# Row dot products in one VectorE instruction at another pace, attention weights turned by transpositions, a convolution begun earlier

## The chip, the cores and the metric

The kernel runs on one core of a Trainium2 chip, as one program from the first load to the last store. The core has four computing engines: TensorE (PE in the profile, its weight loads PEld), VectorE (DVE), ScalarE (ACT) and GpSimd (POOL). SyncE (SP) issues most of the loads. Each engine runs its own instructions in program order and waits on semaphores for the others. The metric is the device time of one execution in microseconds (us), lower is better. Three runs of the kernel before took 2879.74, 2887.54 and 2888.85 us. All order of work is written out by hand: an engine's instructions run in the order in which the code issues them.

## The reference, cut to what matters

Two transformer blocks work one after the other on 512 tokens of width 1024, in float32. The change touches the attention and the convolution of block 1 and the expert layer of block 2.

```python
# block 1, per row of the grid and head: attention over 512 local and 256 context keys
p = softmax(concatenate([s_loc, s_ctx], axis=-1))            # 768 weights for each query
o = einsum('bhqk,bhkd->bhqd', p[..., :n_loc], v_blk) + einsum('bhqk,bhkd->bhqd', p[..., n_loc:], v_ctx)
...
# block 1, conformer convolution: 512 channels, 31 taps over the positions
u = a * sigmoid(g)
y = conv(u, conv_w, width 31, one filter per channel) + conv_b
y = silu(layernorm(y, ln_g, ln_b)) @ w_out
...
# block 2, expert layer: 8 heads x 16 = 128 experts per token out of 16384
u = expert_down[eb]                                          # eb: (tokens, 8, 16)
act = gelu(einsum('td,thkd->thk', xb, u)) * gb
out = einsum('thk,thkd->td', act, expert_up[eb])
```

## The kernel before

**Block 1, attention (`attention1`).** Queries stand in 16 pieces, four pairs of heads by four times 128 positions; the loop over them is `seq`, its counter `n`. For each piece TensorE forms the products (tiles `loc`, `cxs`), VectorE adds the bias and finds the least value (`least`), ScalarE takes the exponentials with their sums into `s1` (`exps`), and then the 128 x 768 weights `P` of each of the two heads have to be turned, six blocks of 128 x 128, into `PT` (`turn`), before TensorE multiplies them with the values (`pv`). The division by the sum is done in the turn: `diag` makes a diagonal matrix `d` of the reciprocals on VectorE, and each block is multiplied with `d` as a float32 matrix product. Between these steps TensorE is kept full by `fill1` (for `n` under 8: the convolution's eight inputs `glu(m)` and units of a modulation product, `m1`) and `fill2` (for `n` from 8). Inputs 0 to 3 of `glu` are the four groups of 128 channels of `a` (tile `u`), 4 to 7 the same groups of `g` (tile `g`).

**Block 1, convolution (`conv_steps`).** It runs on VectorE alone, four channel groups by 31 taps, one instruction of 128 x 512 per tap. It is started at `n == 8` by `glu_end` (four sigmoids on ScalarE between two changes of its function table, four products on VectorE) and then doled out, some seven taps per `n`, and in `merge` some nine per column block of `fill3`. `merge` calls `conv.finish()` at its column block 12; the layer norm behind it (`layernorm`) begins with sums over `y`, the convolution's output in tile `g`, on TensorE (helper line L241).

**Block 2, expert layer (`do_peer`).** Of the four groups of 128 tokens three are computed densely: TensorE forms the products of 384 tokens with all expert rows (`score_steps`, tile `pS`, 102 of 128 chunks stored away to memory, `spill`), weights `wH` and `wL` being the two float32r parts of a loaded float32 tile (`Splitter`: `wH` is a copy on ScalarE, L180, `wL` a subtraction, L189, on VectorE or, where `self.sp.low` is "g", on POOL). The fourth group is gathered: each token's 128 rows of `expert_down` are fetched by number, one indirect DMA of 128 rows (one per partition) at a time, into four buffers `rows`, and multiplied with the token's own row `ht` to a dot product. `Gather.tick` does one step of that: POOL issues the fetch of row `n`, multiplies row `n - 2` with `ht` (L2275), and ScalarE sums row `n - 3` (L2278). After 128 rows, `Gather.up` fetches rows of `expert_up` and adds them up on VectorE (L2301).

The layer has three stages. In the **routing stage** (1522 to 1812 us of the trace) TensorE forms the queries and 47 score chunks, while VectorE sorts the best keys (`Route`, tiles `hv`, `oh`, `pf`) for a budget of microseconds per chunk; ticks begin when the first head's row numbers are known. In the **one-hot stage** (1812 to 2185 us) VectorE makes 96 pairs of one-hot matrices `oo` (L2064, two buffers), ScalarE scales them by the gates (L2068), TensorE multiplies them to `pg` (L2084), and the remaining chunks are scored in between; `spent` counts microseconds and calls a tick when its budget is used up. In the **sum stage** (2185 to 2852 us) TensorE multiplies the weighted scores (`A`, split into `AH` and `AL`) with `expert_up` into `acc`; what is left of the gathering is spread evenly over it by `gpace`, which is computed from the ticks already made.

Of the kernel before, what the change touches and what calls it, by code (L numbers as in the profile page):

```python
# [19 lines left out]
T = 512  # L20
# [265 lines left out]
class Kern:  # L286
# [225 lines left out]
    def b1_plan(self):  # L512
# [6 lines left out]
        for m in range(8):  # L519
            self.fill1 += [("in", 12 + m), ("m1", 8 + m)]  # L520
# [277 lines left out]
    def attention1(self, h, qT, kT, v, u_t, g_t, gA, conv, sm):  # L798
# [3 lines left out]
        with tc.tile_pool(name="a1", bufs=1) as a1, tc.tile_pool(name="ps2", bufs=1, space=PSUM) as ps:  # L802
            def glu(m):
                return self.dmaj_steps(("in", 6 + m // 2), h, ps, lambda pt: nc.scalar.copy(
                    u_t[:, m, 15:15 + T] if m < 4 else g_t[:, m - 4], pt))

            def glu_end():
                for m in range(4):
                    nc.scalar.activation(g_t[:, m], g_t[:, m], AF.Sigmoid)
                    V.tensor_tensor(out=u_t[:, m, 15:15 + T], in0=u_t[:, m, 15:15 + T], in1=g_t[:, m], op=OP.mult)  # L810
                nc.scalar.preload_act_table_set("natural_log_exp_and_others")
# [47 lines left out]
            def diag(Ps):  # L859
                ds = []  # L860
                for P, s1 in Ps:
                    V.tensor_tensor(out=s1[:, 2:3], in0=s1[:, 0:1], in1=s1[:, 1:2], op=OP.add)
                    V.reciprocal(s1[:, 3:4], s1[:, 2:3])
                    d = a1.tile([128, 128], F32, name="d", tag="d", bufs=2)
                    V.tensor_scalar(d, self.c("ident"), s1[:, 3:4], None, op0=OP.mult)
                    ds.append(d)
                return ds

            def turn(Ps, ds, fill):

                PTs = []
                for (P, s1), d in zip(Ps, ds):
# [4 lines left out]
                    for c0, c1 in ((0, 4), (4, 6)):  # L877
                        t1 = ps.tile([128, 4, 128], F32, name="t1", tag="tr", bufs=2)
                        for c in range(c0, c1):
                            nc.tensor.matmul(t1[:, c - c0], P[:, c * 128:(c + 1) * 128], d, start=c == c0,  # L880
                                             stop=c == c1 - 1, skip_group_check=True)
# [15 lines left out]
            ds = diag(Ps)  # L897
            for n, (hp, i) in enumerate(seq):
# [10 lines left out]
                PTs = turn(Ps, ds, fill)  # L909
# [3 lines left out]
                if n == 8:  # L913
                    glu_end()
                if n > 8:
                    conv.run(2.4)
                pv(hp, i, PTs)
                if nxt:
                    ds = diag(Ps)
# [3 lines left out]
                if n > 8:  # L923
                    conv.run(2.4)
# [952 lines left out]
    def do_peer(self):  # L1877
# [7 lines left out]
        with ExitStack() as es:  # L1885
# [39 lines left out]
            with ExitStack() as e2:  # L1925
                rt = e2.enter_context(tc.tile_pool(name="rt2", bufs=1))
                i1, i2, gt = [rt.tile([128, 4, 128], F32, name=n) for n in ("i1", "i2", "gt")]
                with ExitStack() as e3:
# [61 lines left out]
                    while True:  # L1990
# [3 lines left out]
                        if s[0] == "d":  # L1994
# [5 lines left out]
                            if s[1] % 6 < 5:  # L2000
# [35 lines left out]
            with ExitStack() as e3:  # L2036
# [11 lines left out]
                def spent(us):  # L2048
# [3 lines left out]
                    if wait > 0:  # L2052
                        G.tick()
                        wait -= 3.7
# [190 lines left out]
class Gather:  # L2245
# [19 lines left out]
    def tick(self):  # L2265
# [7 lines left out]
        if 2 <= n < 130:  # L2273
            u = self.rows[:, (n - 2) % R]
# [249 lines left out]
```

## Time and profile before

| What | Value |
|---|---|
| median of three runs | 2887.54 us |
| the profiled execution, its own time | 2876.13 us |
| its span in the trace | 2874.3 us |
| PE busy | 2687.1 us (93%) |
| DVE busy | 1759.0 us (61%) |
| ACT busy | 1149.6 us (40%) |
| POOL busy | 940.9 us (33%) |
| POOL's 128 row products, L2275 | 318.8 us |

The span reaches from the first to the last instruction; the execution's own time is 1.8 us longer, and lies 11.4 us under the median of the runs. Busy times of different engines overlap. A share of the whole span says little here, since the stages have different limits: each is to be looked at by itself.

### The profile page before, as it was taken

What the parts mean: (1) busy time and instruction counts of PE and PEld (TensorE: products, weight loads), DVE (VectorE), ACT (ScalarE), POOL (GpSimd) and SP (SyncE); (2) the same over time, 40 slices, a digit from 0 to 9 for tenths busy, and PEclk for the clock granted to TensorE, in tenths of its full rate; (3) what the DMA queues carried; (4) which work ended last, traced back from release to release, by engine and by line L of the source; (5) the groups of instructions that cost most, each with busy time, mean ns of one, the idle gap of its engine ahead of it and who ended that gap; (6) DMA issues with size and microseconds to landing.
All of it is one profiled execution on the core that took longest, in us unless ns stands there. A gap on an engine that the chain in (4) does not pass through costs nothing.

```text
span 2874.3 us, 38727 instructions
## 1 busy us (share of the span) xinstructions
PE 2687.1 (93%) x14985; PEld 2073.9 (72%) x14985; DVE 1759.0 (61%) x2830; ACT 1149.6 (40%) x2226; POOL 940.9 (33%) x555
## 2 busy tenths in 40 slices
PE   7999989989999998999899988898889999999998
PEld 4877757654454444778778878788889898888886
DVE  5234884343233334344449998979884667887887
ACT  3245423321111113244444444788884433333333
POOL 2031233310000001002337777888883533222221
PEclk9999999999999999999999998999999999999999
DMA  7235653379989993210136556677876778999994
GB/s 292 70 131 175 223 203 132 148 303 383 420 341 404 420 419 147 75 59 30 45 123 208 193 191 216 215 264 268 299 277 234 280 263 304 340 335 328 335 344 163
DMA packets 189675, 689.66 MB, mean 240 GB/s; under 512 B 16560, under 2 KB 91952, under 8 KB 134832
## 3 DMA queue, kind: packets, MB, share of 16 engines
q1 hardware_dynamic: 151696, 546.10, 50.9%
q0 software_dynamic: 37504, 137.90, 13.8%
q10 hardware_dynamic: 288, 3.15, 0.3%
q8 instruction: 119, 1.95, 0.3%
q14 instruction: 68, 0.56, 0.1%
HBM read 637.67 MB, written 49.41 MB: 239 GB/s over the span
## 4 chain that ended last, share of the span: by engine, by line
PE 42%; DVE 12%; ACT 7%; issue 2%; DMA 0%; POOL 0%; DVEq 0%; ACTq 0%; POOLq 0%; SPq 0%
PE acc L328 6%; PE acc L329 6%; PE acc L327 6%; PE pS L329 3%; PE pS L327 3%; PE pS L328 3%; DVE oo L2064 2%; DVE wL L189 2%; ACT oo L2068 2%; PE pt L327 2%; ACT wH L180 2%; PE pt L328 2%; PE pt L329 1%; PE pg L2084 1%; ACT rows L2278 1%
## 5 line engine op out<-in xcount | busy, mean ns | idle before, releaser
L189 DVE TENSOR_TENSOR wL<-ringA,wH 128x1024 fp32r<-128x1024 f32 x277 | 398.1, 1443 | 198.3 <-ACT wH L180 193.4
L189 POOL TENSOR_TENSOR wL<-ringA,wH 128x1024 fp32r<-128x1024 f32 (+1 forms) x82 | 189.1, 2312 | 915.5 <-PE bc L351 529.5
L180 ACT CAST wH<-ringA 128x1024 fp32r<-128x1024 f32 (+1 forms) x359 | 366.1, 1026 | 56.9 <-PE acc L329 16.9
L329 PE MATMUL pS<-hH,wL 128*128 128x384 f32 x1024 | 349.5, 341 | 30.4 <-DVE wL L189 30.4
L327 PE MATMUL pS<-hH,wH 128*128 128x384 f32 x1024 | 357.5, 349 | 0.6 <-ACT gS L1908 0.6
L328 PE MATMUL pS<-hL,wH 128*128 128x384 f32 x1024 | 348.1, 340 | 0.0
L2275 POOL TENSOR_TENSOR rows<-rows,ht 128x1024 f32<-128x1024 f32 x128 | 318.8, 2491 | 4.6 <-DMA rows<-e_dn,idx 2.3
L328 PE MATMUL acc<-wL,AH 128*128 128x512 f32 x768 | 305.2, 397 | 3.1 <-DVE wL L189 3.0
L327 PE MATMUL acc<-wH,AH 128*128 128x512 f32 x768 | 304.9, 397 | 0.6 <-ACT AH L2180 0.6
L329 PE MATMUL acc<-wH,AL 128*128 128x512 f32 x768 | 304.6, 397 | 0.0
L2256 POOL DMA_INDIRECT rows<-e_up,idx x128 | 145.5, 1137 | 407.3 <-DVE ht L2301 391.8
L2256 POOL DMA_INDIRECT rows<-e_dn,idx x128 | 191.9, 1499 | 128.9 <-ACT rows L2278 106.2
L327 PE MATMUL pt<-hH,wH 128*128 128x512 f32 x512 | 215.3, 420 | 10.1 <-ACT hH L393 7.0
L329 PEld LDWEIGHTS pS<-hH,wL 128*128 128x128 f32 x1024 | 195.3, 191 | 33.0 <-DVE wL L189 33.0
L2064 DVE TENSOR_TENSOR oo<-cst,cl 128x1024 f32<-128x1024 f32 x96 | 209.5, 2209 | 6.8 <-PE pg L2084 6.6
L328 PE MATMUL pt<-hL,wH 128*128 128x512 f32 x512 | 205.7, 402 | 2.4 <-DVE hL L379 2.3
L329 PE MATMUL pt<-hH,wL 128*128 128x512 f32 x512 | 205.8, 402 | 0.5 <-DVE wL L189 0.5
L327 PEld LDWEIGHTS pS<-hH,wH 128*128 128x128 f32 x1024 | 195.9, 191 | 2.7 <-ACT gS L1908 0.9
L328 PEld LDWEIGHTS pS<-hL,wH 128*128 128x128 f32 x1024 | 195.7, 191 | 1.7
L2180 ACT CAST AH<-A 128x384 fp32r<-128x384 f32 x128 | 65.8, 514 | 312.1 <-PE acc L328 263.2
L328 PEld LDWEIGHTS acc<-wL,AH 128*128 128x128 f32 x768 | 144.7, 188 | 38.8 <-DVE wL L189 5.0
L329 PEld LDWEIGHTS acc<-wH,AL 128*128 128x128 f32 x768 | 144.8, 189 | 35.3 <-DVE AL L2184 0.3
(496 smaller groups left out, 5241.4 us busy)
## 6 DMA issues: line engine op xcount, KB each, us to landing
ringA<-t_dn SPq DMA_DIRECT2D x64, 1024.0 KB, 5.7
ringA<-t_up SPq DMA_DIRECT2D x64, 1024.0 KB, 7.3
ringB<-w_eu SPq DMA_DIRECT2D x42, 1024.0 KB, 12.8
ringA<-w_ed SPq DMA_DIRECT2D x39, 1024.0 KB, 9.0
ringB<-w_eg SPq DMA_DIRECT2D x37, 1024.0 KB, 13.3
ringA<-w_in SPq DMA_DIRECT2D x30, 1024.0 KB, 5.2
ringA<-w_eg SPq DMA_DIRECT2D x28, 1024.0 KB, 11.0
ringB<-w_ed SPq DMA_DIRECT2D x27, 1024.0 KB, 8.5
```

The lines of the kernel that those rows point to most:

```text
L180: self.kern.nc.scalar.copy(H, v)
L189: (self.kern.nc.vector if self.low == "v" else self.kern.nc.gpsimd).tensor_tensor(out=L, in0=v, in1=H, op=OP.subtract)
L327: te.matmul(ps, a[0], b[0], start=start, stop=False, skip_group_check=skip)
L328: te.matmul(ps, a[0], b[1], start=False, stop=False, skip_group_check=skip)
L329: te.matmul(ps, a[1], b[0], start=False, stop=stop, skip_group_check=skip)
L2064: V.tensor_tensor(out=oo, in0=iota.unsqueeze(1).unsqueeze(1).to_broadcast([128, 2, 4, 128]), in1=cl[:, 0:2, tok:tok + 4].unsqueeze(3).to_b ...
L2068: nc.scalar.activation(oo[:, 0, t], oo[:, 0, t], AF.Copy, scale=cl[:, 2, tok + t:tok + t + 1])
L2084: nc.tensor.matmul(pg[:, t], o2[:, t], o1[:, t], start=True, stop=True)
L2180: nc.scalar.copy(AH, A)
L2256: k.nc.gpsimd.indirect_dma_start(out=self.rows[:, p % self.R], out_offset=None, in_=k.ap[src], in_offset=bass.IndirectOffsetOnAxis(ap=self ...
L2275: nc.gpsimd.tensor_tensor(out=u, in0=u, in1=self.ht, op=OP.mult)
L2278: nc.scalar.activation(u, u, AF.Copy, accum_out=self.S[:, n - 3:n - 2])
```

## The change

1. `Gather.tick` no longer uses POOL and ScalarE for the dot product. One VectorE instruction multiplies row `n - 3` with `ht` and sums it into `S`. POOL keeps the fetches.
2. The ticks come at another pace: in the routing stage with every second score chunk instead of five of six, in the one-hot stage every 4.2 us of counted work instead of 3.7. By the two programs 31, 63 and 34 of the 128 dot products now stand in the routing, one-hot and sum stages; before it were 47, 71 and 10.
3. `diag` is gone. `scaled` divides `P` by its sum in place, on ScalarE, and `turn` uses transpositions (the constant identity `ident` as the moving operand) instead of products with `d`.
4. `fill1` takes the convolution's inputs in the order 0, 1, 4, 5, 2, 3, 6, 7; `glu_end` is called twice, for channel groups 0 and 1 as soon as four inputs are there, for 2 and 3 as soon as eight are. The convolution is doled out from the `n` after the first call.

```diff
-        for m in range(8):
-            self.fill1 += [("in", 12 + m), ("m1", 8 + m)]
+        for m, i in enumerate((0, 1, 4, 5, 2, 3, 6, 7)):
+            self.fill1 += [("in", 12 + i), ("m1", 8 + m)]
...
-            def glu_end():
-                for m in range(4):
+            def glu_end(ms):
+
+                for m in ms:
                     nc.scalar.activation(g_t[:, m], g_t[:, m], AF.Sigmoid)
+                for m in ms:
                     V.tensor_tensor(out=u_t[:, m, 15:15 + T], in0=u_t[:, m, 15:15 + T], in1=g_t[:, m], op=OP.mult)
                 nc.scalar.preload_act_table_set("natural_log_exp_and_others")
...
-            def diag(Ps):
-                ds = []
+            def scaled(Ps):
+
                 for P, s1 in Ps:
                     V.tensor_tensor(out=s1[:, 2:3], in0=s1[:, 0:1], in1=s1[:, 1:2], op=OP.add)
                     V.reciprocal(s1[:, 3:4], s1[:, 2:3])
-                    d = a1.tile([128, 128], F32, name="d", tag="d", bufs=2)
-                    V.tensor_scalar(d, self.c("ident"), s1[:, 3:4], None, op0=OP.mult)
-                    ds.append(d)
-                return ds
+                for P, s1 in Ps:
+                    nc.scalar.activation(P, P, AF.Copy, scale=s1[:, 3:4])
...
-                            nc.tensor.matmul(t1[:, c - c0], P[:, c * 128:(c + 1) * 128], d, start=c == c0,
-                                             stop=c == c1 - 1, skip_group_check=True)
+                            nc.tensor.transpose(t1[:, c - c0], P[:, c * 128:(c + 1) * 128], self.c("ident"))
...
-                if n == 8:
-                    glu_end()
-                if n > 8:
+                if n > first:
                     conv.run(2.4)
+                if (n >= 8 or first > n) and len(glus) >= 4 * (1 + (n >= 8)) and ends:
+                    first = min(first, n)
+                    glu_end(ends.pop(0))
                 pv(hp, i, PTs)
                 if nxt:
-                    ds = diag(Ps)
+                    scaled(Ps)
                 fill.run(0.5 * us)
                 if left == 1:
                     fill.finish()
-                if n > 8:
+                if n > first:
                     conv.run(2.4)
...
-                            if s[1] % 6 < 5:
+                            if s[1] % 2:
                                 G.tick()
...
-                        wait -= 3.7
+                        wait -= 4.2
...
-        if 2 <= n < 130:
-            u = self.rows[:, (n - 2) % R]
-            nc.gpsimd.tensor_tensor(out=u, in0=u, in1=self.ht, op=OP.mult)
         if 3 <= n:
             u = self.rows[:, (n - 3) % R]
-            nc.scalar.activation(u, u, AF.Copy, accum_out=self.S[:, n - 3:n - 2])
+            nc.vector.scalar_tensor_tensor(u, u, 1.0, self.ht, op0=OP.mult, op1=OP.mult,
+                                           accum_out=self.S[:, n - 3:n - 2])
```

The first place is VectorE in the attention loop where the convolution begins. Before, this is at `n` = 9; the rows run from the first tap (L748) to the taps behind `diag` (L862 to L865).

```order
L748 TENSOR_SCALAR g<-u,prm 128x512
L752 SCALAR_TENSOR_TENSOR g<-u,prm,g 128x512 x3
L862 TENSOR_TENSOR s_2229<-s_2229 128x1
L863 RECIPROCAL s_2229<-s_2229 128x1
L865 TENSOR_SCALAR d<-cst,s_2229 128x128
L862 TENSOR_TENSOR s_2232<-s_2232 128x1
L863 RECIPROCAL s_2232<-s_2232 128x1
L865 TENSOR_SCALAR d<-cst,s_2232 128x128
L752 SCALAR_TENSOR_TENSOR g<-u,prm,g 128x512 x4
```

Of the changed kernel the same place stands at `n` = 5; the sums and reciprocals (now L868, L869) are left.

```order
L748 TENSOR_SCALAR g<-u,prm 128x512
L752 SCALAR_TENSOR_TENSOR g<-u,prm,g 128x512 x3
L868 TENSOR_TENSOR s_1760<-s_1760 128x1
L869 RECIPROCAL s_1760<-s_1760 128x1
L868 TENSOR_TENSOR s_1763<-s_1763 128x1
L869 RECIPROCAL s_1763<-s_1763 128x1
L752 SCALAR_TENSOR_TENSOR g<-u,prm,g 128x512 x4
```

The diagonal is gone from VectorE, and the taps begin four pieces earlier; the two scalings of `P` (128 x 768) stand on ScalarE behind the exponentials.

The second place is VectorE in the middle of the one-hot stage. Before, it had only the one-hot matrices and the subtractions of the weights:

```order
L2064 TENSOR_TENSOR oo<-cst,cl 128x1024 x2
L189 TENSOR_TENSOR wL<-ringA,wH 128x1024
L2064 TENSOR_TENSOR oo<-cst,cl 128x1024 x2
L189 TENSOR_TENSOR wL<-ringA,wH 128x1024
L2064 TENSOR_TENSOR oo<-cst,cl 128x1024 x2
```

In the changed kernel the dot products of the gathered rows (L2280) stand among them:

```order
L2280 SCALAR_TENSOR_TENSOR rows,S<-rows,ht 128x1024
L2069 TENSOR_TENSOR oo<-cst,cl 128x1024
L189 TENSOR_TENSOR wL<-ringA,wH 128x1024
L2280 SCALAR_TENSOR_TENSOR rows,S<-rows,ht 128x1024
L2069 TENSOR_TENSOR oo<-cst,cl 128x1024 x2
L189 TENSOR_TENSOR wL<-ringA,wH 128x1024
L2280 SCALAR_TENSOR_TENSOR rows,S<-rows,ht 128x1024
L2069 TENSOR_TENSOR oo<-cst,cl 128x1024
```

About two of three one-hot matrices now have a dot product next to them on VectorE.

The third place is POOL in the routing stage, where it has fetches and, for every second chunk, a subtraction. Of the changed kernel:

```order
L2261 DMA rows<-e_dn,idx 128x1024 x2
L189 TENSOR_TENSOR wL<-ringA,wH 128x1024
L2261 DMA rows<-e_dn,idx 128x1024 x2
L189 TENSOR_TENSOR wL<-ringA,wH 128x1024
L2261 DMA rows<-e_dn,idx 128x1024 x2
```

And before, with a product behind each fetch:

```order
L2256 DMA rows<-e_dn,idx 128x1024
L2275 TENSOR_TENSOR rows<-rows,ht 128x1024
L189 TENSOR_TENSOR wL<-ringA,wH 128x1024
L2256 DMA rows<-e_dn,idx 128x1024
L2275 TENSOR_TENSOR rows<-rows,ht 128x1024
L2256 DMA rows<-e_dn,idx 128x1024
L2275 TENSOR_TENSOR rows<-rows,ht 128x1024
```

The products are gone from POOL; in the one-hot stage nothing but fetches is left there.

## Rows read from the trace of the kernel before

**Rows 1.** Busy time by stretch: start:end, length, PE, PEld, DVE, ACT, POOL, clock, DMA share, GB/s

```profile
140.00:345.00 205.00, 201.86 (x1658) 147.88 (x1654) 107.60 (x287) 100.44 (x276) 41.95 (x21) 1.00 0.46 159
345.00:400.00 55.00, 54.48 (x361) 39.54 (x364) 53.37 (x49) 20.87 (x43) 24.86 (x11) 1.00 0.76 285
400.00:450.00 50.00, 37.21 (x216) 24.34 (x209) 27.08 (x32) 11.32 (x23) 8.43 (x4) 0.86 0.47 167
1522.00:1812.00 290.00, 259.58 (x1376) 245.07 (x1375) 274.54 (x776) 132.57 (x210) 231.11 (x112) 0.95 0.62 210
1812.00:2185.00 373.00, 325.59 (x1986) 308.77 (x1985) 310.02 (x155) 309.00 (x737) 302.12 (x149) 0.98 0.76 263
2400.00:2852.00 452.00, 452.00 (x1958) 366.49 (x1957) 356.91 (x419) 161.13 (x223) 98.56 (x100) 1.00 0.92 322
```

**Rows 2.** What TensorE waited for in these stretches: total us, times, longest

```profile
PE cs L241 <- DVE g L752: 12.8, 1, 12.8
...
PE pS L329 <- DVE wL L189: 30.4, 8, 10.9
...
PE pg L2084 <- ACT oo L2068: 41.0, 44, 2.9
PE t L2031 <- DVE i L2407: 6.2, 2, 5.6
```

**Rows 3.** Timeline of VectorE and POOL around 1612 us: start, duration

```profile
1612.33 3.54 DVE L189 TENSOR_TENSOR wL<-ringA,wH 128x1024 fp32r<-128x1024 f32 x1
...
1612.37 2.41 POOL L2275 TENSOR_TENSOR rows<-rows,ht 128x1024 f32<-128x1024 f32 x1
```

**Rows 4.** VectorE's groups, routing stage (two), one-hot stage (two): busy us, mean ns

```profile
L189 DVE TENSOR_TENSOR wL<-ringA,wH 128x1024 fp32r<-128x1024 f32 x33 | 59.2, 1806 | 14.0 <-ACT wH L180 13.8 <-issue 0.3
L2404 DVE TENSOR_TENSOR oh<-oh,hif 128x1024 f32<-128x1024 f32 x14 | 27.4, 1996 | 0.0
...
L2064 DVE TENSOR_TENSOR oo<-cst,cl 128x1024 f32<-128x1024 f32 x96 | 209.5, 2209 | 6.8 <-PE pg L2084 6.6
L189 DVE TENSOR_TENSOR wL<-ringA,wH 128x1024 fp32r<-128x1024 f32 x51 | 94.9, 1863 | 52.2 <-ACT wH L180 52.2
```

**Rows 5.** Single lines of the code: min/median/max ns, first and last start

```profile
L2064 DVE TENSOR_TENSOR oo<-cst,cl x96: 1210/1216/4016, 1821.5 to 2167.7; 128x1024 f32<-128x1024 f32 x96
...
L189 POOL TENSOR_TENSOR wL<-ringA,wH x21: 2373/2407/3887, 1524.9 to 1805.9; 128x1024 fp32r<-128x1024 f32 x21
```

**Rows 6.** The same view, for lines like the new dot product

```profile
L1289 DVE SCALAR_TENSOR_TENSOR junk<-srow,cst,grow x32: 741/748/753, 630.2 to 1072.9; 128x512 f32<-128x512 f32 x32
L1289 DVE DVE_READ_ACCUMULATOR junk<-srow,cst,grow x32: 80/84/86, 630.9 to 1073.5; 128x1 f32 x32
...
L2301 DVE SCALAR_TENSOR_TENSOR ht<-rows,S,ht x127: 1276/1279/1287, 2266.2 to 2823.5; 128x1024 f32<-128x1024 f32 x127
```

**Rows 7.** The same view, ScalarE's sum of a row and its exponentials

```profile
L2278 ACT ACTIVATE rows<-rows x128: 1042/1062/1081, 1526.1 to 2259.3; 128x1024 f32<-128x1024 f32 x128
...
L854 ACT ACTIVATE P<-P,m x32: 721/727/740, 141.5 to 328.6; 128x512 f32<-128x512 f32 x32
```

**Rows 8.** Timeline of TensorE: six products with `d`; later eight transpositions in block 2

```profile
158.15 1.60 PE L880 MATMUL t<-d,P 128*128 128x128 f32 x12
159.51 0.47 PE L327 MATMUL pt<-hH,wH 128*128 128x512 f32 x1
...
1253.75 1.03 PE L1663 MATMUL t<-cst,P 128*128 128x128 f32 x8
1254.62 0.28 PE L1643 MATMUL S<-negu,idb 128*128 128x128 bf16 x2
```

**Rows 9.** Convolution taps on VectorE: group from 336 to 424 us, then all

```profile
L752 DVE SCALAR_TENSOR_TENSOR g<-u,prm,g 128x512 f32<-128x512 f32 x82 | 83.9, 1023 | 2.9
...
L752 DVE SCALAR_TENSOR_TENSOR g<-u,prm,g x120: 741/752/2956, 266.1 to 423.3; 128x512 f32<-128x512 f32 x120
```

**Rows 10.** DMA issues, 1522 to 2185 us: count, median us to landing

```profile
rows<-e_dn,idx POOLq DMA_INDIRECT x119, 5.6
```

## What was predicted

> **What bounds the kernel now.** I read the busy times by stretch first, then what TensorE waited for in each, then the instructions that were late. The stretches of [rows 1] show where TensorE is the limit: it is busy 201.9 of 205 us in the attention of block 1 and all 452 us of the sum stage. There only less work for TensorE can help. In three stretches it idles. From 400 to 450 us it works 37.2 us at a mean clock of 0.86; one single wait, of 12.8 us, is named in [rows 2], for the convolution's last tap. In the routing stage it idles 30.4 us, all of it for the subtractions `wL` on VectorE, which is busy 274.5 of 290 us. In the one-hot stage it idles 47.2 us, 41.0 of them for ScalarE's scaled one-hots `oo` and 6.2 for the last routing step.
>
> Why VectorE is so full is seen in [rows 3]: a subtraction begins at 1612.33 us, POOL's product of a gathered row at 1612.37, and the subtraction takes 3.54 us, while lines of its kind and size take 1.2 us alone [rows 5]. It ends about one subtraction after POOL's product does. In [rows 4] the whole groups are stretched: the one-hots of L2064 take 2209 ns in the mean against a median of 1216 for the same line [rows 5] (its worst is 4016), the subtractions 1806 and 1863, the routing's products 1996. So POOL's product doesn't only cost POOL: while it runs, VectorE's instructions with two operands in on-chip memory stand still.
>
> **The change part by part.** *The turn.* A piece's six products with `d` are twelve passes of TensorE; from their start to that of the next instruction it is 159.51 - 158.15 = 1.36 us [rows 8]. Eight transpositions in block 2 take 1254.62 - 1253.75 = 0.87 us, 0.109 each, so six take 0.65. There are 32 turns: 32 x 0.71 = 22.7 us less, on an engine with 98% of this stretch, if the weights are ready. They are now scaled on ScalarE, 128 x 768. No such row exists: 512 columns take 0.73 us, 1024 take 1.06 [rows 7]; I take 0.9 each, 29 us in all, on an engine with 100.4 busy of 205 [rows 1]. The scaling waits for `pv`, the sum and the reciprocal, and is followed by half of the filling work and the next products on TensorE, some 4 us by the stretch's pace (205 us over 16 pieces is 12.8 each); it hides there except at the first piece and where the function table is changed once more. I charge 3 us; from below nothing, from above 0.7 us for each of the 32 turns, which would eat the gain. Sum: -20.
>
> *The convolution* begins four pieces earlier. Seven taps a piece at 0.75 us [rows 9] are 21 us of VectorE's work moved into a stretch where it is busy 107.6 of 205. Before, it is full (53.4 of 55 us) while TensorE comes to the layer norm, and 82 taps took 83.9 us there, 1023 ns each. The layer norm is reached 20 us earlier, but 29 taps fewer are left behind the attention, 29 x 1.02 = 30 us, on top of which VectorE no longer makes `d`. 30 is more than 20, but less than 20 + 12.8, so by this sum 2.8 us of the wait would stay; VectorE's lag at the attention's end is gone too, so I count the wait as removed, -12.8. From below -10; from above -15, since the clock's fall goes with the idle time.
>
> *Routing stage.* Of the 68 long POOL instructions (47 products, 21 subtractions [rows 5]) 47 go. The two groups of this stage in [rows 4] are stretched by 33 x (1.806 - 1.216) + 14 x (1.996 - 1.216) = 30.4 us; 47/68 of that is 21.0. VectorE gets 31 dot products. Their price: a line of the same operation with a sum, 512 wide, takes 748 ns and 84 more to read the sum out; the same operation without a sum, 1024 wide, takes 1279 [rows 6]. So 1.36 us each, 42.2 us. VectorE: 274.5 - 21.0 + 42.2 = 295.7, which is 6 us more than the stage has now. That bound leaves out the smaller groups that are stretched as well. The other bound is that all TensorE's waits go, -30.4. I take the middle, -12.
>
> *One-hot stage.* POOL is left with fetches. The two groups are stretched by 96 x 0.993 + 51 x 0.647 = 128.3 us; 63 dot products cost 85.7. VectorE: 310.0 - 128.3 + 85.7 = 267.4 us. ScalarE loses 71 sums of 1.06 us, of 309.0. Both are then well under TensorE's own 325.6 us, so I count its whole idle time as gone: -47. From above half of it, -24, if the two one-hot buffers keep the three engines in step; from below -60, since TensorE's 325.6 includes filling its pipeline again behind some 46 waits.
>
> *Sum stage.* 24 more dot products and 24 more fetches land here, and the pace rises from (259 - 121)/150 + 0.02 = 0.94 to (259 - 97)/150 + 0.02 = 1.10 steps a chunk. VectorE is busy 357 of 452 us; 0.16 x 1.3 us a chunk over some 107 chunks add 22, to 84%. The DMA's share is 0.92 at 322 GB/s; 0.16 fetches of 0.52 MB a chunk add 9 MB to 145.5, 6%, to 0.98. Both are covered by TensorE's full 452 us: 0. If transfers were full already, 6% of 452 would be 27 us more; that is the upper end.
>
> Together -20 - 12.8 - 12 - 47 = -92. From the profiled execution's 2876.1 that gives 2784; the runs' median lies 11.4 us above that execution, so I predict 2796 for the runs.
>
> **A rule against it.** The new line has two float32 operands in on-chip memory and a sum, and [rows 6] show this form 512 wide at 748 ns, as fast per column as the form without a sum (752 ns [rows 9]). The Trainium skill's page Vector Engine (DVE) Microarchitecture Reference, section Points that are easy to get wrong, says that this operation with two sources in SBUF that aren't bf16 runs at half throughput, as no port is left for the accumulator. By that rule a dot product would take about twice as long; the trace disagrees, and the sum goes by the trace.
>
> **The rivals.** *VectorE stays the bound* in routing (+6) and the one-hot stage gives only half (-24): -33 + 6 - 24 = -51, 2837. For it speaks the sum of 295.7, against it the stretched groups left out. *The scaling comes late at every turn* and eats the 20 us: -72, 2816. For it: ScalarE is in order, and what it does for the filling work stands behind a scaling that waits for VectorE. Against: four microseconds of cover. *The dot product costs double*, 2.64 us: routing 274.5 - 21 + 81.8 = 335, +45; one-hot 310 - 128.3 + 166.3 = 348, -25; in all -13, 2875. Against it speak the 748 ns. *Slower: VectorE now waits for the gather.* It is in order, so a dot product whose row hasn't landed holds the subtractions and one-hots behind it; before, POOL stood there and held nobody on TensorE's path. 94 dot products lie in the two stages; at 0.98 us of wait each the 92 us are gone, at 1.5 us it is +49, 2937. Against it: a fetch lands 5.6 us after its issue [rows 10], and is issued three ticks ahead, some 15 us in the one-hot stage (63 ticks in 326 us). *Better:* routing -30, one-hot -60, 2765. That the row's sum on ScalarE was what TensorE waited for, and not POOL's hold, changes nothing, as both go.
>
> **How the numbers follow.** Forecast 0.60 (2768 to 2815), VectorE stays the bound 0.18, scaling late 0.12, double cost 0.02, late gather 0.04, better 0.04. The range 2768 to 2842 holds the forecast and the first two rivals and leaves out what is beyond. 0.3%, some 9 us, is what runs of this kernel spread and so about what a measurement tells from no change. Faster by more than that: 0.94, within it 0.02, slower 0.04.
>
> **What would show it.** In the profile after: L880's successor at 0.65 us for six transpositions; no wait of L241 for a tap; the one-hots' mean near 1.22 us and `wL` on VectorE near 1.23 in the one-hot stage; TensorE's wait for `oo` under 10 us; the dot product near 1.28 us plus 0.08. The prediction is wrong if the routing stage is longer than 290 us, if VectorE's idle time is put down to the landing of gathered rows, or if the sum stage shows TensorE waiting.

## The result and the profile after

The changed kernel takes 2783.34 us in the median of four runs (2781.31 to 2786.41), the kernel before, on the same chip, 2883.64 (2875.05 to 2888.85): a ratio of 0.9659, 95% interval 0.9633 to 0.9685. The forecast was 2796 us, within 2768 to 2842, and faster. The profiled execution took 2781.99 us with a span of 2780.1, which is 94 us less than before's 2874.3.

The first view is that of [rows 1] for the kernel after, over the stretches that answer to those (all start earlier now); the sixth stretch is the sum stage.

```profile
140.00:340.00 200.00, 185.91 (x1471) 127.39 (x1469) 124.25 (x284) 130.04 (x313) 42.17 (x23) 0.97 0.47 164
340.00:400.00 60.00, 59.87 (x388) 43.81 (x389) 51.02 (x45) 22.02 (x45) 25.44 (x12) 1.00 0.79 288
400.00:450.00 50.00, 49.32 (x309) 34.86 (x309) 7.53 (x16) 19.27 (x38) 9.91 (x6) 1.00 0.50 176
1500.00:1768.00 268.00, 255.58 (x1368) 242.01 (x1367) 257.93 (x837) 85.94 (x120) 97.44 (x53) 0.97 0.58 200
1768.00:2090.00 322.00, 312.19 (x2002) 305.04 (x2001) 252.57 (x284) 234.94 (x593) 107.15 (x65) 0.99 0.83 290
2306.00:2758.00 452.00, 448.60 (x1928) 361.97 (x1927) 371.94 (x429) 159.66 (x222) 126.50 (x115) 1.00 0.94 336
```

Against [rows 1], the one-hot stage (fifth row) leaves TensorE 10 us of idle time instead of 47, and the stretch from 400 to 450 us, where the layer norm falls, is full at a clock of 1.00 instead of 37.2 us at 0.86. In the routing stage (fourth row) VectorE is still the fuller engine, 257.9 of 268 us. The first row went the other way: TensorE had been at 201.9 of 205 us in the attention, and now stands for 14 of 200, at a clock of 0.97.

The second view is what TensorE waited for in the kernel after, first from 136 to 430 us, then from 1460 to 2250 us: total us, times, longest. It answers to [rows 2].

```profile
PE pt L553 <- ACT gA L820: 3.2, 3, 1.3
PE t L884 <- ACT P L871: 3.0, 1, 3.0
PE cxs L893 <- ACT P L861: 2.9, 4, 1.0
...
PE pS L329 <- DVE wL L189: 12.4, 5, 4.7
PE pg L2089 <- ACT oo L2073: 7.0, 13, 2.9
PE t L2036 <- DVE i L2410: 2.3, 2, 1.6
```

The wait of 12.8 us for a tap is gone, that for the scaled one-hots fell from 41.0 to 7.0, that for the subtractions from 30.4 to 12.4. New are small waits for ScalarE in the attention, one of 3.0 us for the scaled weights (L871).

The third view is of single lines of the kernel after, the new dot product, its sum, the one-hots and the scaling: min/median/max ns. It answers to [rows 5] and [rows 6].

```profile
L2280 DVE SCALAR_TENSOR_TENSOR rows<-rows,ht x128: 1200/1218/3421, 1518.6 to 2241.6; 128x1024 f32<-128x1024 f32 x128
L2280 DVE DVE_READ_ACCUMULATOR rows<-rows,ht x128: 76/83/87, 1519.7 to 2242.8; 128x1 f32 x128
...
L2069 DVE TENSOR_TENSOR oo<-cst,cl x96: 1215/1220/1226, 1775.6 to 2071.3; 128x1024 f32<-128x1024 f32 x96
...
L871 ACT ACTIVATE P<-P,s x32: 919/935/977, 145.9 to 330.5; 128x768 f32<-128x768 f32 x32
```

The worst one-hot now takes 1.23 us, where it was 4.02; a dot product takes 1.22 + 0.08 us.

Where the time went is read best from instructions that both kernels have. The table gives, for each kernel below, how many us later (+) or earlier (-) than in before's profile six of them stand: the end of the last product with `v` in the attention (341.1 us before), the end of the layer norm's last mean `cs` (426.1), the first product `pS` of the routing stage (1490.4), the first one-hot (1821.5), the first product `acc` of the sum stage (2216.0), the end of the span (2874.3).

| kernel | attention ends | layer norm | routing begins | one-hots begin | sum begins | end |
|---|---|---|---|---|---|---|
| after | -5.5 | -20.2 | -21.5 | -45.9 | -95.7 | -94.2 |
| e1_gather | -1.2 | -1.3 | -4.0 | -11.8 | -53.8 | -57.7 |
| e2_gather_pace | +0.9 | +0.8 | +1.4 | -23.5 | -72.5 | -72.7 |
| e3_turn | -5.6 | -4.2 | -1.1 | +5.7 | +4.1 | +7.2 |
| e4_conv | +1.3 | -13.4 | -15.3 | -18.5 | -18.7 | -18.7 |
| e5_pool_product | -7.4 | -22.1 | -17.3 | +0.5 | +24.2 | +69.4 |
| e6_act_sum | -6.2 | -20.9 | -19.5 | +13.2 | -14.4 | -13.8 |
| e7_double | -7.9 | -22.6 | -23.6 | -9.9 | -10.9 | -0.7 |
| e8_scale_early | -9.0 | -23.7 | -21.9 | -46.4 | -96.8 | -96.6 |
| e9_no_sum | +1.3 | +1.9 | +1.1 | +0.5 | -18.5 | -21.2 |
| e10_no_product | +1.1 | +0.9 | -2.1 | -42.2 | -95.8 | -100.1 |
| e11_scale_vectore | -18.0 | -32.7 | -26.6 | -51.2 | -101.3 | -101.7 |
| e12_pace_third | -12.6 | -27.3 | -24.5 | -53.2 | -103.1 | -104.8 |

The difference of two neighbouring columns is what a stage gave. One profile is behind each row, and it is no exact measure: e3_turn has before's routing code, and its routing stage came out 6.8 us longer (-1.1 to +5.7). The medians of the runs decide where some us matter.

### The profile page after: what moved, and what is told of

Same layout as the page of the kernel before. It is cut to its first block, busy times and chain, and to the rows that moved or that the text cites. A ratio compares the mean times of both kernels' runs of the same rounds, so it can differ in the third digit from the quotient of the medians.

```text
span 2780.1 us, 38313 instructions
## 1 busy us (share of the span) xinstructions
PE 2649.8 (95%) x14793; PEld 2044.7 (74%) x14793; DVE 1695.4 (61%) x3054; ACT 1047.4 (38%) x2004; POOL 632.1 (23%) x427
## 4 chain that ended last, share of the span: by engine, by line
PE 41%; DVE 10%; issue 6%; ACT 3%; POOL 2%; DMA 1%; DVEq 0%; POOLq 0%; ACTq 0%; SPq 0%
PE acc L329 5%; PE acc L327 5%; PE acc L328 5%; PE pS L327 3%; PE pS L329 3%; PE pS L328 3%; PE pg L2089 2%; PE pt L327 2%; POOL rows L2261 2%; PE pt L328 2%; PE pt L329 2%; DVE rows L2280 1%; DVE wL L189 1%; DVE oo L2069 1%; PE gu L1323 1%
## 5 line engine op out<-in xcount | busy, mean ns | idle before, releaser
L189 DVE TENSOR_TENSOR wL<-ringA,wH 128x1024 fp32r<-128x1024 f32 x277 | 339.5, 1231 | 186.4 <-ACT wH L180 182.7
L329 PE MATMUL pS<-hH,wL 128*128 128x384 f32 x1024 | 347.6, 339 | 12.4 <-DVE wL L189 12.4
L2261 POOL DMA_INDIRECT rows<-e_dn,idx x128 | 200.4, 1565 | 447.9 <-DVE rows L2280 409.5
L2261 POOL DMA_INDIRECT rows<-e_up,idx x128 | 151.4, 1183 | 333.2 <-DVE ht L2304 309.2
L327 PEld LDWEIGHTS acc<-wH,AH 128*128 128x128 f32 x768 | 145.1, 189 | 35.0 <-ACT AH L2185 1.0
L2304 DVE SCALAR_TENSOR_TENSOR ht<-rows,S,ht 128x1024 f32<-128x1024 f32 x127 | 162.5, 1280 | 3.3 <-DMA rows<-e_up,idx 2.6
## 6 DMA issues: line engine op xcount, KB each, us to landing
ringB<-w_eu SPq DMA_DIRECT2D x42, 1024.0 KB, 12.9
```

Source lines behind the costliest of these rows:

```text
L189: (self.kern.nc.vector if self.low == "v" else self.kern.nc.gpsimd).tensor_tensor(out=L, in0=v, in1=H, op=OP.subtract)
L327: te.matmul(ps, a[0], b[0], start=start, stop=False, skip_group_check=skip)
L329: te.matmul(ps, a[1], b[0], start=False, stop=stop, skip_group_check=skip)
L2261: k.nc.gpsimd.indirect_dma_start(out=self.rows[:, p % self.R], out_offset=None, in_=k.ap[src], in_offset=bass.IndirectOffsetOnAxis(ap=self ...
L2304: V.scalar_tensor_tensor(self.ht, u, self.S[:, p:p + 1], self.ht, op0=OP.mult, op1=OP.add)
```

## The experiments

The kernel before took, beside them, 2879.75 us in the median for the first four, 2879.36 for the next four, 2877.68 for the last four. All ratios are to it.

**One part at a time.** The theory: the parts add, VectorE freed from POOL's hold is the largest. The rival: VectorE, with the dot products on it, stays what TensorE waits for. *e1_gather* is the kernel before with the dot product on VectorE and the old paces:

```diff
-        if 2 <= n < 130:
-            u = self.rows[:, (n - 2) % R]
-            nc.gpsimd.tensor_tensor(out=u, in0=u, in1=self.ht, op=OP.mult)
         if 3 <= n:
             u = self.rows[:, (n - 3) % R]
-            nc.scalar.activation(u, u, AF.Copy, accum_out=self.S[:, n - 3:n - 2])
+            nc.vector.scalar_tensor_tensor(u, u, 1.0, self.ht, op0=OP.mult, op1=OP.mult,
+                                           accum_out=self.S[:, n - 3:n - 2])
```

> The kernel before with the dot product moved to VectorE alone, at the old pace of ticks (five of six chunks, 3.7 us). If POOL's product was what held VectorE, this alone brings nearly all of the 74 us that the routing and one-hot stages gained, less what the denser dot products cost: 16 more in the routing stage at 1.3 us each, so routing -5 to -24 and one-hot -45 to -55, in all -55 to -75 us. If the new pace is what pays, under -40 us.

Measured: 2822.59 us, ratio 0.9789 (0.9765 to 0.9812). The routing stage gave 7.8 us, the one-hot stage 42.0, a little under the 45 expected. So the dot product's new place brings most of the gain at the old pace already.

*e2_gather_pace* adds the new paces:

```diff
-                            if s[1] % 6 < 5:
+                            if s[1] % 2:
...
-                        wait -= 3.7
+                        wait -= 4.2
```

> The dot product on VectorE at the new pace, block 1 as before. By the sum of the two traces -74 us (routing -24, one-hot -50, sum stage +1). If the two halves of the change help each other (an earlier block 1 moves the loads), it differs from that by over 8 us.

Measured: 2803.05 us, 0.9713 (0.9688 to 0.9739). Now routing gave 24.9 us and one-hot 49.0, and the sum stage, which took 24 dot products more, grew no longer (-0.2 us). So the pace is worth about 20 us: 16 dot products fewer in routing make 17 us there.

*e3_turn* is before with the transpositions and ScalarE's scaling alone:

```diff
-                    d = a1.tile([128, 128], F32, name="d", tag="d", bufs=2)
-                    V.tensor_scalar(d, self.c("ident"), s1[:, 3:4], None, op0=OP.mult)
...
+                for P, s1 in Ps:
+                    nc.scalar.activation(P, P, AF.Copy, scale=s1[:, 3:4])
...
-                            nc.tensor.matmul(t1[:, c - c0], P[:, c * 128:(c + 1) * 128], d, start=c == c0,
-                                             stop=c == c1 - 1, skip_group_check=True)
+                            nc.tensor.transpose(t1[:, c - c0], P[:, c * 128:(c + 1) * 128], self.c("ident"))
```

> Only the turn: weights scaled on ScalarE, blocks transposed, convolution begun as before. If the scaling on ScalarE costs the turn's gain by itself, the attention is 0 to 6 us shorter as in the changed kernel, and the layer norm's wait grows by as much: about 0 in all. If it is the earlier convolution beside it that makes the scaling late, the attention is 15 to 22 us shorter; the wait for the last tap then takes it back, since VectorE's taps aren't earlier: 0 to -8 in all.

Measured: 2873.61 us, 0.9973 (0.9954 to 0.9992), 6 us by the medians; its span of 2881.6 us is of a longer run. The attention ends 5.6 us earlier, as in the whole change, so the convolution isn't what holds it up; the wait for the tap is back with 14.2 us.

*e4_conv* is before with the new order in `fill1` and `glu_end` in two calls, weights turned as before:

```diff
-        for m in range(8):
-            self.fill1 += [("in", 12 + m), ("m1", 8 + m)]
+        for m, i in enumerate((0, 1, 4, 5, 2, 3, 6, 7)):
+            self.fill1 += [("in", 12 + i), ("m1", 8 + m)]
...
-                if n == 8:
-                    glu_end()
-                if n > 8:
+                if n > first:
                     conv.run(2.4)
+                if (n >= 8 or first > n) and len(glus) >= 4 * (1 + (n >= 8)) and ends:
+                    first = min(first, n)
+                    glu_end(ends.pop(0))
```

> Only the convolution begun earlier, the turn by products with the diagonal as before. The wait of 12.8 us for the last tap goes: -12 to -16 us, the attention itself 0 to 3 us longer. If the changed attention's losses come from the earlier taps, the attention is 8 us longer or more and the whole is -5 or less.

Measured: 2862.39 us, 0.993 (0.9902 to 0.9957). By the medians that is 17.4 us, a little more than the 12 to 16 expected. The layer norm's means end 13.4 us earlier and stand behind no tap. The stretch behind them is no longer at the low clock either: in before the granted clock is 1.2 GHz for 13.7 us from 415.3 us on, while TensorE waits for the tap and just after; in e4 it stays at 2.4 GHz there.

By the medians *e2_gather_pace* gave 76.7 us, *e3_turn* 6.1 and *e4_conv* 17.4. Together that is 100.2, where the whole change gave 100.3: the parts add.

**What made the groups slow: POOL's product or ScalarE's sum.** The change takes both away. *e5_pool_product* adds to the kernel after a product on POOL that nobody reads, *e6_act_sum* a sum on ScalarE that nobody reads, each behind the dot product:

```diff
             nc.vector.scalar_tensor_tensor(u, u, 1.0, self.ht, op0=OP.mult, op1=OP.mult,
                                            accum_out=self.S[:, n - 3:n - 2])
+            nc.gpsimd.tensor_tensor(out=u, in0=u, in1=self.ht, op=OP.mult)
```

```diff
+        self.S2 = pool.tile([128, 1], F32, name="S2")
...
             nc.vector.scalar_tensor_tensor(u, u, 1.0, self.ht, op0=OP.mult, op1=OP.mult,
                                            accum_out=self.S[:, n - 3:n - 2])
+            nc.scalar.activation(u, u, AF.Copy, accum_out=self.S2)
```

> The changed kernel, with a POOL product of the same size put behind each dot product; it multiplies a row that is already summed, in place, and nobody reads the result. If POOL's product holds VectorE, the one-hots' mean goes back from 1.2 to about 2.2 us and the two stages lose most of their 74 us: +50 to +80 us. If what counted was the work on the path (ScalarE's sum, POOL's product before it), it costs under 15 us.

> The changed kernel, with ScalarE's sum of a row (1.06 us and 0.19 to read the sum) put behind each dot product, its result unread. If ScalarE's relief was what paid in the one-hot stage, +30 us or more, with TensorE's wait for the scaled one-hots back at 30 to 40 us. If POOL's hold on VectorE was it, 0 to +12 us.

Measured: 2938.66 us for e5, 1.0204 (1.0168 to 1.0241), and 2863.49 for e6, 0.9945 (0.9928 to 0.9962), 155 and 80 us over the kernel after. The first is more than either theory said. The second, by its time alone, speaks for ScalarE, though the wait for the scaled one-hots came back with 17.3 us and not with 30 to 40. Its trace says what the time is made of. These are e6's waits from 1460 to 2250 us, of ScalarE and then of TensorE:

```profile
ACT rows L2283 <- DVE rows L2281: 224.8, 70, 11.0
...
PE pt L327 <- ACT wH L180: 20.9, 7, 4.4
PE pg L2089 <- ACT oo L2073: 17.3, 39, 3.5
```

ScalarE stood 224.8 us at the added sum until VectorE had made the dot product, with the casts `wH` and the one-hots' scaling queued behind it. So e6 priced a wait that I had added, not the sum. e5 has the same fault: POOL's product waits 238.8 us for VectorE's, with the subtractions on POOL behind it, and TensorE waits 40.9 us for those. The one-hots' mean does go up in e5, from 1220 to 1643 ns, and stays at 1219 in e6, but by their times neither run decides.

The clean pair takes one piece of work away from the kernel before, with nothing behind VectorE. *e9_no_sum* leaves the sum out, so the factors `S` are a constant; *e10_no_product* leaves the product out, so that ScalarE sums the row as fetched:

```diff
-        if 3 <= n:
-            u = self.rows[:, (n - 3) % R]
-            nc.scalar.activation(u, u, AF.Copy, accum_out=self.S[:, n - 3:n - 2])
+        if n == 0:
+            nc.gpsimd.memset(self.S, 0.01)
```

```diff
-        if 2 <= n < 130:
-            u = self.rows[:, (n - 2) % R]
-            nc.gpsimd.tensor_tensor(out=u, in0=u, in1=self.ht, op=OP.mult)
```

> The kernel before with ScalarE's sum of each gathered row left out (the factors S are a constant; POOL's product stays). If POOL's product holds VectorE, the stretched groups stay at 1.8 to 2.2 us and the time falls by 0 to 12 us. If what TensorE waited for was ScalarE, with 71 sums of 1.06 + 0.19 us in the one-hot stage, it falls by 35 us or more and the wait for the scaled one-hots goes from 41 us to under 12.

> The kernel before with POOL's product of each gathered row left out (ScalarE sums the row as it was fetched). If POOL's product holds VectorE, the subtractions and one-hots on VectorE come to means of 1.2 to 1.3 us and the time falls by 60 to 85 us. If ScalarE's sums are the limit, it falls by 20 us or less.

Measured: 2851.54 us for e9, 0.9892 (0.986 to 0.9924), and 2777.26 for e10, 0.9645 (0.9617 to 0.9674): 26 and 100 us by the medians. The groups of VectorE's subtractions and one-hots over the whole span, in e9:

```profile
L189 DVE TENSOR_TENSOR wL<-ringA,wH 128x1024 fp32r<-128x1024 f32 x277 | 380.0, 1376 | 183.5 <-ACT wH L180 178.9 <-PE t L1663 2.6 <-DMA sd<-gS 0.9
L2064 DVE TENSOR_TENSOR oo<-cst,cl 128x1024 f32<-128x1024 f32 x96 | 219.1, 2319 | 1.8 <-ACT cl L2033 0.9 <-PE pg L2084 0.8
```

and in e10:

```profile
L189 DVE TENSOR_TENSOR wL<-ringA,wH 128x1024 fp32r<-128x1024 f32 x277 | 339.6, 1231 | 280.2 <-ACT wH L180 275.0 <-PE t L1663 2.6 <-DMA gS<-sd 0.4
L2064 DVE TENSOR_TENSOR oo<-cst,cl 128x1024 f32<-128x1024 f32 x96 | 114.7, 1220 | 16.5 <-PE pg L2084 11.7 <-DMA sd<-gS 4.7
```

Without the sum the one-hots stay at 2319 ns (2209 in [rows 4]); without the product they are at 1220, as in the kernel after. TensorE's waits from 1460 to 2250 us say the same, in e9:

```profile
PE pS L329 <- DVE wL L189: 28.7, 8, 8.1
PE pg L2084 <- ACT oo L2068: 26.3, 25, 2.9
```

and in e10, with all of ScalarE's sums still there:

```profile
PE pg L2084 <- ACT oo L2068: 7.3, 5, 5.4
...
PE pS L329 <- DVE wL L189: 0.7, 1, 0.7
```

So POOL's product was the cause, in both stages. ScalarE's sum had a share in the one-hot stage alone (19.0 us there in e9, 0.6 in routing), and e9's 26 us lie between the two figures expected. Without the product, TensorE waits only 7.3 us for the scaled one-hots with all the sums still there, so little of that share can be left; a kernel without either wasn't run. e10 gains more than the 85 us expected, as its routing stage gives 40.1 us: the 30.4 us of waits went, and the clock of that stage rose from 0.95 to 1.00.

**What a dot product costs on VectorE.** *e7_double* makes each twice:

```diff
+        self.S2 = pool.tile([128, 1], F32, name="S2")
...
             nc.vector.scalar_tensor_tensor(u, u, 1.0, self.ht, op0=OP.mult, op1=OP.mult,
                                            accum_out=self.S[:, n - 3:n - 2])
+            nc.vector.scalar_tensor_tensor(u, u, 1.0, self.ht, op0=OP.mult, op1=OP.mult, accum_out=self.S2)
```

> The changed kernel with each dot product made twice on VectorE, the second result unread: 31, 63 and 34 instructions of 1.3 us more in the three stages, 40, 82 and 44 us. If VectorE bounds the routing stage, that stage takes +25 to +40 us; if TensorE bounds the one-hot stage with VectorE at 253 of 322 us, that stage takes +5 to +35 us (the 82 us have only 70 us of room); the sum stage 0 to +5. In all +30 to +75 us.

Measured: 2881.63 us, 0.9998 (0.9983 to 1.0012), 98 us over the kernel after. By the table, against after, routing is 38.1 us longer for 31 more dot products, one-hot 48.8 for 63, the sum stage 8.7 for 34: 1.23, 0.78 and 0.26 us each, of the 1.30 that each takes. Only the routing stage is within what was expected; the other two, and the whole, are over it. Its waits of TensorE from 1460 to 2250 us:

```profile
PE pg L2089 <- ACT oo L2073: 41.0, 32, 2.9
PE pS L329 <- DVE wL L189: 36.9, 13, 8.2
```

VectorE is busy 327.5 of 393 us in e7's one-hot stage, so it has room by the sum; but a one-hot that stands behind two dot products in its queue is late all the same: ScalarE's wait for the one-hots grows from 67.3 us in after to 116.5.

**Where the turn's gain went.** Of 20 us forecast for the turn, 5.5 came. From one piece's product with `v` to the next, the kernel before takes 12.8 to 13.6 us in pieces 1 to 8, after 11.4 to 13.2; then two pieces of after take 16.0 and 14.2 us, where before takes 12.9 and 10.9. They are slow in two ways. In the first, ScalarE's copy of a finished product out of the accumulator (`gA`) stands behind the scaling in its queue, and TensorE waits 1.32 us for the place that this copy frees, after a wait of 1.04 us for late exponentials shortly before; the granted clock is then 1.2 GHz from 264.4 to 271.2 us:

```profile
261.99 1.76 ACT L871 ACTIVATE P<-P,s 128x768 f32<-128x768 f32 x2 [0.26 <-DVE s L868]
263.66 0.56 ACT L820 COPY gA<-pt 128x512 f32<-128x512 f32 x1
264.27 1.85 PE L553 MATMUL pt<-ringA,cs 128*32 128x256 f32 x16 [1.32 <-ACT gA L820]
```

In the second, the scaling itself is late. This is after's timeline there, lines of ScalarE, VectorE, SyncE and TensorE in order of time:

```profile
274.70 0.33 SPq L116 DMA_DIRECT2D ringA<-w_in  x1
...
276.57 0.40 ACT L558 COPY modsb<-pt 128x256 f32<-128x256 f32 x1
...
278.21 0.16 DVE L869 RECIPROCAL s<-s 128x1 f32<-128x1 f32 x1
...
281.33 1.99 ACT L180 CAST wH<-ringA 128x1024 fp32r<-128x1024 f32 x2 [4.36 <-DMA ringA<-w_in]
283.23 1.76 ACT L871 ACTIVATE P<-P,s 128x768 f32<-128x768 f32 x2
284.22 0.93 PE L884 MATMUL t<-cst,P 128*128 128x128 f32 x6 [2.99 <-ACT P L871]
```

Both factors for the scaling are there at 278.37 us, but the scaling stands behind a cast of filling work, and the cast waits 4.36 us for its weights. So it begins at 283.23, and TensorE stands 2.99 us; from 284.9 to 288.3 us its clock is at 1.2 GHz again. Before, `d` was made on VectorE, and the cast's wait, 3.14 us there, held nothing of the turn. *e8_scale_early* places the scaling ahead of the products with `v`:

```diff
-                pv(hp, i, PTs)
                 if nxt:
                     scaled(Ps)
+                pv(hp, i, PTs)
```

> The changed kernel with the sums, reciprocals and scalings issued before the piece's last products (pv) instead of behind them, so that ScalarE doesn't stand at a scaling until TensorE and VectorE are through with that. If ScalarE's standing there ate the turn's gain, the attention gets 8 to 15 us shorter and the whole is -8 to -15 us. If POOL's subtractions on VectorE's small sums (1.9 us for one of 0.15) or the table changes are it, under -4 us.

Measured: 2776.58 us, 0.9638 (0.9619 to 0.9657). The attention ends 3.5 us earlier than after's; the two pieces stay slow (16.2 and 14.8 us): TensorE still waits 1.48 us for the copy `gA`, and this place of the scaling is still behind the cast, which now waits 4.97 us. The time, 6.8 us under after's by the medians and 2.4 by the profiles, lies between the two figures expected. *e11_scale_vectore* is e8 with the scaling on VectorE from piece 8 on:

```diff
-                    nc.scalar.activation(P, P, AF.Copy, scale=s1[:, 3:4])
+                    if late:
+                        V.tensor_scalar(P, P, s1[:, 3:4], None, op0=OP.mult)
+                    else:
+                        nc.scalar.activation(P, P, AF.Copy, scale=s1[:, 3:4])
...
-                    scaled(Ps)
+                    scaled(Ps, n >= 8)
```

> The change with the scaling ahead of the products with v, as in e8_scale_early, and from piece 8 on made by VectorE. If what made pieces 9 to 11 of block 1 slow is that the scaling stands in ScalarE's queue behind a cast that waits for a transfer of w_in (4.97 us in e8_scale_early), TensorE's wait of 3.6 us and the fall of its clock go, the attention ends 6 to 10 us earlier than in e8_scale_early, and the time is 2766 to 2771 us. If the pieces are slow for the transfers themselves, or VectorE's taps come late instead, it stays within 3 us of e8_scale_early's 2776.6.

Measured: 2774.23 us, 0.9634 (0.9609 to 0.9659). The attention ends 9.0 us earlier than e8's, 18.0 earlier than before's, and the two pieces take 11.4 and 11.6 us. Busy time and clock from 258 to 292 us, as in [rows 1], in after:

```profile
258.00:292.00 34.00, 28.64 (x230) 19.14 (x232) 24.97 (x55) 18.64 (x51) 5.14 (x2) 0.85 0.44 156
```

and in e11:

```profile
258.00:292.00 34.00, 32.10 (x319) 21.36 (x315) 32.14 (x67) 18.42 (x57) 5.15 (x2) 1.00 0.63 221
```

TensorE idled 5.4 us of these 34 in after, and its granted clock was 0.85 of 2.4 GHz in the mean, as it was at 1.2 GHz for 10.2 us of them. In e11 it idles 1.9 us, and the fall is gone, though the cast still waits 5.13 us for its weights. So the scaling's place in ScalarE's queue is shown as the cause, and not the late transfer by itself. By its time e11 is only 2.4 us under e8, as the rival expected: 4.3 of the 9 us are given back between the layer norm and the routing stage, most of it around 780 us, where TensorE is at 1.2 GHz for 13.7 us (6.8 in e8). Why that fall got longer stays open.

*e12_pace_third* is e11 with fewer steps of the gather in routing:

```diff
-                            if s[1] % 2:
+                            if s[1] % 3 == 1:
```

> As e11_scale_vectore, with a step of the gather behind every third group of the routing stage's spills in place of every second, so some seven dot products more lie in the sum stage. If VectorE is still what TensorE waits for in routing (22 us of waits for subtractions), 3 to 9 us less than e11_scale_vectore; if the sum stage has no room left (VectorE 372 of 452 us, transfers at 0.94), the same or up to 9 us more.

Measured: 2768.61 us, 0.9613 (0.9589 to 0.9638); its runs (2766.88 to 2771.28) all lie under e11's (2771.88 to 2777.89). Routing gives 28.7 us instead of 24.6, and the sum stage takes the seven further dot products without growing. (The 22 us of waits in its expectation are TensorE's for everything in the two stages of after; those for the subtractions are 12.4.) It is the fastest of the kernels that compute all of the reference. Its attention is 5.4 us longer than e11's with the same code: the transfer of `w_in` holds the cast 7.49 us here, and TensorE stands 4.27 us for the turned weights, whose copy from the accumulator is ScalarE's as well. The scaling is off that queue, the copy isn't; what makes the transfer take that long wasn't tried.

## Why the prediction was right, and where its terms were off

- *The sum*: -92 forecast, -94.2 in the profile. It is right in part because two errors meet: the attention gave 14.5 us less than its term, routing 12.4 more. The medians fell by 100, since after's runs lie 1.4 us above its profiled execution and not the 11.4 that the forecast added; that is 10 of the 13 us between forecast and result.
- *The turn*: -20 forecast, -5.5 measured. The price of the transpositions held (six mostly take 0.57 or 0.63 us, where 0.65 was taken), and the scaling takes 0.935 us where 0.9 was taken. The step that failed is "it hides there except at the first piece and where the function table is changed once more. I charge 3 us". In its place, the scaling held a copy that TensorE needed in one piece, and stood behind a cast that waited for a transfer in the next; e11, with the later scalings on VectorE, gets 18.0. The rival *the scaling comes late at every turn* came nearest, in size and engine, but it isn't every turn: of the 12.5 us that e11 gives back, 7.2 are in these two pieces and the clock's fall there. A busy share of 100 of 205 us for ScalarE had said nothing on where it stands still.
- *The convolution*: -12.8 forecast; from the attention's end to the layer norm's means after gains 14.7 us, e4 alone 14.7 too. Right.
- *Routing*: -12 forecast, -24.4 measured. Mis-sized was what POOL's hold costs VectorE: "47/68 of that is 21.0". From before's routing stage to e10's, VectorE's busy time falls by 61.2 us (315.3 to 254.1). The two groups counted give 32.3 of it, about all of the stretch of 30.4 although POOL's subtractions are still there, so the share of 47/68 was wrong; the rest is in the groups left out, 22.7 of it in three of instructions with one operand (casts and an operation with a scalar, L2382, L2398, L2400). The stage gave 40.1 us by e10, and the other bound, the 30.4 us of waits, left the clock of 0.95 out. The dot products take the 42.2 us of VectorE that were forecast (254.1 in e10 to 296.4 in after), but the stage grew by only 15.7 us from e10 to after, 0.5 for each of the 31; only the second 31, in e7, come near their full price.
- *One-hot stage*: -47 forecast, -49.8 measured; the mechanism is right, the size in part by luck. Of "so I count its whole idle time as gone" 37.6 us came: TensorE's idle time went from 47.4 to 9.8 us. The other 13.4 us between the stretches of 373 and 322 us are TensorE's own busy time, 325.6 against 312.2 with about as many matmuls (1986 and 2002), which the step held fixed and the prediction named only as its lower bound. What shortened it wasn't tried. The step has little to spare, too: e7 shows that VectorE at 83% brings back 41 us of waits.
- *Sum stage*: 0 forecast, +1.5 measured, with the transfers at 0.94 instead of the 0.98 worked out. Right in size; but TensorE, which waited for nothing there before, now waits 3.4 us for the part `AL` of the weighted scores, which VectorE makes: one of the signs that the prediction named for being wrong.
- *The rivals*: *VectorE stays the bound* fell by its prices (+6 and -24, where -24.4 and -49.8 came); true of it is that VectorE is still the fuller engine in routing, busy 257.9 of 268 us, and e12 gets 4.1 us there for seven dot products fewer. *Late gather* fell: VectorE waits 0.8 us once in 128 dot products for a row, though a fetch now lands 6.8 us after its issue where [rows 10] have 5.6. *The dot product costs double* fell: 1218 ns for 1024 columns, against 748 for 512 in [rows 6]. The rule of the Trainium skill's page Vector Engine (DVE) Microarchitecture Reference, section Points that are easy to get wrong, isn't what this case's trace shows for this form.
- That POOL's product, and not ScalarE's sum, was what held the stages had been left open; e9 and e10 settle it.

## What to carry to other kernels

Where VectorE's groups have a mean far above their median, look for what POOL runs at that moment: here moving 319 us of POOL's products onto VectorE as 169 us of work of its own made VectorE less busy in the two stages that mattered. Before a step is put on an engine because it has time, list what stands ahead of it in that engine's queue and what each of those waits for, a transfer above all, and what will then stand behind it. And price a suspect by taking it away from the kernel before; an unread copy added behind another engine's result measures the wait for that result.

## What was unexpected of the hardware

POOL's hold takes small instructions too. In after's timeline, VectorE's second sum of two columns of one element each starts just behind the first of a pair of POOL's subtractions:

```profile
327.52 0.15 DVE L868 TENSOR_TENSOR s<-s 128x1 f32<-128x1 f32 x1
327.70 0.16 DVE L869 RECIPROCAL s<-s 128x1 f32<-128x1 f32 x1
327.78 2.37 DVE L868 TENSOR_TENSOR s<-s 128x1 f32<-128x1 f32 x1
330.19 0.16 DVE L869 RECIPROCAL s<-s 128x1 f32<-128x1 f32 x1
330.27 2.75 DVE L752 SCALAR_TENSOR_TENSOR g<-u,prm,g 128x512 f32<-128x512 f32 x1
...
327.75 4.72 POOL L189 TENSOR_TENSOR wL<-ringA,wH 128x1024 fp32r<-128x1024 f32 x2 [40.16 <-ACT wH L180]
```

It takes 2.37 us instead of the 0.15 of the first sum, about one of the two subtractions; the reciprocal with one operand takes its 0.16 us while the second subtraction runs, and the next tap, with two large operands, is held again (2.75 instead of 0.75 us). This is as the Trainium skill's page SBUF — State Buffer, section Who interferes with whom, has it: an instruction of VectorE with two inputs in SBUF and one of POOL that reads SBUF keep each other out for a whole instruction. Here an operand of one column was held as long as one of 1024.

One operand doesn't always save an instruction either, though the prediction speaks of two. In before's routing stage, casts and an operation with a scalar that read one tile were held as well (shortest, median, longest):

```profile
L2398 DVE TENSOR_SCALAR pu<-tp x16: 180/184/2437, 1508.7 to 1808.7; 128x64 uint32<-128x64 uint32 x16
...
L2400 DVE CAST pf<-pu x16: 182/195/5427, 1509.7 to 1808.9; 128x64 f32<-128x64 uint32 x16
...
L2382 DVE CAST hif<-hi x8: 228/1404/3360, 1499.8 to 1790.0; 128x128 f32<-128x128 uint32 x8
```

The longest of the last line starts at 1742.42 us, inside a product of POOL (1740.91, 2.42 us), and ends at 1745.78, with POOL's next subtraction (1743.28, 2.41 us). The reductions of L2407 took 1.20 or 1.21 us beside POOL's products too.
